# A 31-tap convolution as 8-phase Toeplitz matmuls through DRAM scratch, with batched LayerNorm and a block-wise first phase

## Chip, cores, metric

One Trainium2 chip, all 8 cores, each running the same program on its own share: one prompt sequence of 2048 positions and 16 of the 128 sample requests (4 tokens each), 2112 columns a core in blocks of 512, 512, 512, 512 and 64. The time of a run is the device time of its slowest core, in microseconds (us). Some executions of any kernel here fall into a slower state, in which the cores of one die show a lower granted TensorE clock; only fast runs are compared below.

## The reference, cut

Two layers; each is RMSNorm, one input projection into 56 column tiles of 128, two groups of 8 heads, one output projection, residual. The change concerns group A:

```python
def hybrid_layer(x, buf_a, buf_b, norm_g, w_in, conv_a_w, conv_a_b, ln_a_g, ln_a_b, conv_b_w, w_out):
    h = rmsnorm(x, norm_g)
    p = jnp.einsum('btd,de->bte', h, w_in)                           # (B, T, D_IN)
    # [cut: split into a_val, a_gate, z_a, gb, gc, hb, z_b]
    # group A: Conformer convolution module
    u = a_val * jax.nn.sigmoid(a_gate)                               # GLU
    ca, new_a = causal_dwconv(u, buf_a, conv_a_w)                    # width 31, depthwise
    ca = head_layernorm(ca + conv_a_b, ln_a_g, ln_a_b)               # over 128 channels, per token
    y_a = jax.nn.silu(ca) * jax.nn.silu(z_a)
    # [cut: group B, short convolution of width 3 with gates]
    y = jnp.einsum('bte,ed->btd', jnp.concatenate([y_a, y_b], axis=-1), w_out)
    return x + y, new_a, new_b
```

## The kernel before, as far as the change touches it

Channels are on partitions and positions along the free dimension. Each engine runs its operations in the order in which the program lists them; a helper turns the listed reads and writes into semaphore waits. `pop_rank` and `defer` place the later stages of one step among the matmuls of the next.

```python
def a_step(l, j, b, jj, slots):                 # one head j, one block b
    mm_group(bg, n, [... w_gate, h ...]); pop_rank(1)            # g projection, 8 matmuls
    # ... tanh on ScalarE, v projection, u = (tanh+1)*v on VectorE into ubuf ...
    mm_group(bz, n, [... w_z, h ...])                            # z projection
    # ... silu(z) on ScalarE ...
    def pe_fn(e):                                                # taps 12..30: diagonal matmuls
        for i, k in enumerate(pe_taps):
            ins = e.matmul(banks[bd][:, 0:n], lhsT=mk[:, ms, k, :], rhs=usl(k), start=(i == 0), ...)
    def dve_taps(k0, k1):                                        # taps 0..11: multiply-adds on VectorE
        # ... two chains of scalar_tensor_tensor over usl(k) ...
    def stage0():   # two merges on TensorE with the centring matrix cb16; Square on ScalarE
    def stage1():   # variance: matmul with ones
    def stage2():   # Ln, Exp on ScalarE; tt = (centred + bias) * rstd on VectorE
    def stage3():   # s = silu(gain*tt + bias) on ScalarE
    def stage4():   # y = s * silu(z) on VectorE
    for rk, fn in enumerate([stage0, stage1, stage2, stage3, stage4]):
        defer(sid, rk, fn)
# [cut: start: x in blocks; every block normalised before the first projection]
# [cut: 4 output rounds a layer, 4 heads each]
```

## Time and profile before

| | before |
|---|---|
| median (fast runs) | 1615.1 us (1614.3 to 1616.2, 4 runs) |
| spans of the cores | 1606.2 to 1615.4 us |
| mean granted TensorE clock by core | 0.962 to 0.973 |
| TensorE busy, VectorE busy | 1433 us, 1229 us |
| table loads on ScalarE | 165 |

The engine totals, the groups and the unbroken runs of matmuls are shown in the prediction. Two further lines of the page: the granted clock in forty equal slices, in tenths of full speed, and the traffic.

```profile
PEclk9999999999999999999989999999999999999997
...
HBM read 92.20 MB, written 13.37 MB: 65 GB/s over the span
```

The clock was nearly full throughout, 0.97 in the mean on this core. To compare kernels I also took the start of every matmul of one core from the trace. The gap to the next start, less the cost of that matmul when it runs unbroken (0.216 us for 512 columns, 0.1425 for 336, 0.029 for 64, all from the prediction; the middle one is an estimate there), is what a wait or a cold clock added. Before, on core 3: 10.1 us ahead of the first matmul + 1363.6 of matmul by count + 222.1 added + 19.6 after the start of the last one = 1615.4 us.

### The profile page before, as it was taken

What the parts mean: (1) busy time and instruction counts of PE and PEld (TensorE: products, weight loads), DVE (VectorE), ACT (ScalarE), POOL (GpSimd) and SP (SyncE); (2) the same over time, 40 slices, a digit from 0 to 9 for tenths busy, and PEclk for the clock granted to TensorE, in tenths of its full rate; (3) what the DMA queues carried; (4) which work ended last, traced back from release to release, by engine and by line L of the source; (5) the groups of instructions that cost most, each with busy time, mean ns of one, the idle gap of its engine ahead of it and who ended that gap; (6) DMA issues with size and microseconds to landing.
All of it is one profiled execution on the core that took longest, in us unless ns stands there. A gap on an engine that the chain in (4) does not pass through costs nothing.

```text
span 1615.4 us, 23509 instructions; the slowest of 8 cores (1606.2 to 1615.4 us)
## 1 busy us (share of the span) xinstructions
PE 1433.3 (89%) x7642; PEld 652.0 (40%) x7642; DVE 1229.2 (76%) x2240; ACT 622.8 (39%) x896; POOL 78.6 (5%) x148
## 2 busy tenths in 40 slices
PE   2399998999999999999979999899998999999983
PEld 0144443444444444444434444444444444444431
DVE  1589998899896556655699999889998665655566
ACT  2346665266652111111245666436665111011133
POOL 1000000000000010010000000000000010000000
PEclk9999999999999999999989999999999999999997
DMA  7801111111112131122411011111111222113116
GB/s 191 190 12 22 26 27 20 33 27 27 21 20 37 27 53 27 27 42 38 39 33 20 12 22 26 21 33 27 26 21 20 37 34 46 27 27 53 21 38 184
DMA packets 43253, 65.91 MB, mean 41 GB/s; under 512 B 14016, under 2 KB 16320, under 8 KB 43072
## 3 DMA queue, kind: packets, MB, share of 16 engines
q0 software_dynamic: 20736, 37.76, 14.7%
q1 hardware_dynamic: 22400, 26.67, 6.5%
q8 instruction: 64, 1.05, 0.3%
q14 instruction: 53, 0.43, 0.1%
HBM read 92.20 MB, written 13.37 MB: 65 GB/s over the span
## 4 chain that ended last, share of the span: by engine, by line
PE 73%; issue 9%; DVE 8%; ACT 5%; DMA 4%; SPq 1%; DVEq 0%; ACTq 0%
PE psb L360 58%; PE psb L517 13%; DMA x_sb<-xT 3%; ACT L563 2%; DVE h_sb L404 1%; DVE acc L538 1%; PE psb L550 1%; ACT rstd_t L565 1%; DVE vbuf L630 1%; ACT lnv_t L563 1%; DVE accb L538 1%; DVE y_sb L578 1%; ACT sq L382 1%; PE psb L389 1%; DVE acc L535 1%
## 5 line engine op out<-in xcount | busy, mean ns | idle before, releaser
L360 PE MATMUL psb<-h_sb,wsl 128*128 128x512 bf16 (+1 forms) x4480 | 839.4, 345 | 19.8 <-DVE vbuf L630 12.0
L360 PEld LDWEIGHTS psb<-h_sb,wsl 128*128 128x128 bf16 x4480 | 381.0, 98 | 456.0 <-issue 42.7
L538 DVE SCALAR_TENSOR_TENSOR acc<-ubuf,cwh,acc 128x512 f32<-128x512 bf16 (+1 forms) x640 | 371.1, 652 | 0.5 <-DVE acc L538 0.3
L517 PE MATMUL psb<-ubuf,mk 128*128 128x512 bf16 (+1 forms) x1520 | 289.5, 346 | 12.7 <-DVE ubuf L479 7.5
L360 PE MATMUL psb<-y_sb,wsl 128*128 128x512 bf16 (+1 forms) x1280 | 250.9, 355 | 14.2 <-DVE x_sb L429 6.1
L429 DVE TENSOR_TENSOR x_sb<-x_sb,psb 128x512 f32<-128x512 f32 (+1 forms) x320 | 181.2, 592 | 43.6 <-PE psb L360 41.6
L517 PEld LDWEIGHTS psb<-ubuf,mk 128*128 128x128 bf16 x1520 | 129.8, 99 | 161.8 <-issue 21.7
L630 DVE TENSOR_TENSOR vbuf<-psb,tt_t 128x512 bf16<-128x512 f32 (+1 forms) x80 | 47.7, 597 | 164.9 <-PE psb L360 164.9
L360 PEld LDWEIGHTS psb<-y_sb,wsl 128*128 128x128 bf16 x1280 | 112.1, 100 | 148.5 <-issue 40.4
L616 ACT ACTIVATE sz_t<-psb 128x512 f32<-128x512 f32 (+1 forms) x80 | 41.9, 523 | 284.2 <-PE psb L360 284.2
L574 ACT ACT_TABLE_LOAD x80 | 102.6, 1283 | 85.7 <-DVE tt_t L567 85.7
L471 ACT ACTIVATE th_t<-psb 128x512 f32<-128x512 f32 (+1 forms) x80 | 41.8, 523 | 228.6 <-PE psb L360 228.4
L623 ACT ACTIVATE tt_t<-psb 128x512 f32<-128x512 f32 (+1 forms) x80 | 41.8, 523 | 210.7 <-PE psb L360 203.0
L654 DVE SCALAR_TENSOR_TENSOR acc<-vbuf,cw_b_sb,acc 128x512 f32<-128x512 bf16 (+1 forms) x160 | 105.3, 658 | 17.4 <-DVE acc L651 0.9
L563 ACT ACT_TABLE_LOAD x80 | 102.6, 1283 | 23.5 <-PE psb L360 21.7
L343 POOL DMA_DIRECT2D wsl<-w_in_r x112 | 61.0, 556 | 970.5 <-PE psb L360 947.0
L538 DVE SCALAR_TENSOR_TENSOR accb<-ubuf,cwh,acc 128x512 bf16<-128x512 bf16 (+1 forms) x160 | 97.7, 652 | 0.0
L389 PE MATMUL psb<-sq,ones_s 128*128 128x512 bf16 (+1 forms) x120 | 38.2, 426 | 56.1 <-ACT sq L382 56.0
L382 ACT ACTIVATE sq<-x_sb 128x1024 bf16<-128x1024 f32 (+1 forms) x60 | 51.5, 898 | 79.0 <-PE psb L389 35.9
L404 DVE SCALAR_TENSOR_TENSOR h_sb<-x_sb,vecs_sb,rstd_t 128x512 bf16<-128x512 f32 (+1 forms) x80 | 46.5, 654 | 42.2 <-ACT rstd_t L397 42.1
L550 PE MATMUL psb<-accb,cb 128*128 128x512 bf16 (+1 forms) x160 | 44.7, 345 | 36.3 <-DVE accb L538 36.3
L567 DVE SCALAR_TENSOR_TENSOR tt_t<-psb,cbias,rstd_t 128x512 f32<-128x512 f32 (+1 forms) x80 | 52.4, 655 | 24.6 <-ACT rstd_t L565 24.2
(44 smaller groups left out, 714.3 us busy)
## 6 DMA issues: line engine op xcount, KB each, us to landing
wsl<-w_in_r POOLq DMA_DIRECT2D x112, 256.0 KB, 5.5
x_sb<-xT SPq DMA_DIRECT2D x4, 2048.0 KB, 31.8
wsl<-w_out_r POOLq DMA_DIRECT2D x32, 256.0 KB, 4.4
y_fm<-sz_t SPq DMA_DIRECT2D x18, 256.0 KB, 2.2
hista<-hist_a SPq DMA_DIRECT2D x16, 240.0 KB, 2.6
y_fm<-th_t SPq DMA_DIRECT2D x14, 256.0 KB, 2.2
oa_copy<-sa_orig SPq DMA_DIRECT2D x2, 1664.0 KB, 23.0
oa_new<-oa_t SPq DMA_DIRECT2D x2, 256.0 KB, 12.6
```

Source lines behind the costliest of these rows:

```text
L343: P.op("pool", (lambda e, i=i, s=s: e.dma_start(out=wsl[:, s, :], in_=wseq[i])), reads=([x_r[0][0]] if i == 0 else []), writes=[w_r[s]], c ...
L360: ins = e.matmul(outap, lhsT=l_, rhs=r_, start=(i == 0), stop=(i == len(pairs) - 1))
L382: P.op("act", (lambda e, s=s, kp=kp, c0=c0, n=n: e.activation(out=sq[:, s, :, 0:n], in_=x_sb[:, 2 * kp:2 * kp + 2, c0:c0 + n], func=AF.Squ ...
L404: P.op("dve", (lambda e, k=k, c0=c0, n=n: e.scalar_tensor_tensor(out=h_sb[:, k, c0:c0 + n], in0=x_sb[:, k, c0:c0 + n], scalar=vecs[:, gcol ...
L429: P.op("dve", (lambda e, bk=bk, m=m, c0=c0, n=n: e.tensor_tensor(out=x_sb[:, m, c0:c0 + n], in0=x_sb[:, m, c0:c0 + n], in1=banks[bk][:, 0: ...
L517: ins = e.matmul(banks[bd][:, 0:n], lhsT=mk[:, ms, k, :], rhs=usl(k), start=(i == 0), stop=(nd == 0 and i == len(pe_taps) - 1))
L538: P.op("dve", (lambda e, k=k, wcol=wcol, outap=outap, c=c: e.scalar_tensor_tensor(out=outap, in0=usl(k), scalar=wcol, in1=acc[:, c, 0:n], ...
L550: P.op("pe", (lambda e, c=c, ci=ci: e.matmul(banks[bd][:, 0:n], lhsT=cb16[:], rhs=accb[:, 2 * iac + c, 0:n], start=False, stop=(ci == len( ...
L563: P.op("act", (lambda e: e.activation(out=lnv_t[:, 0, 0:n], in_=banks[bvv][:, 0:n], func=AF.Ln, bias=LN_EPS)), reads=[bank_r[bvv]], writes ...
L574: P.op("act", (lambda e: e.activation(out=ss_t[:, 0, 0:n], in_=tt_t[:, 0, 0:n], func=AF.Silu, scale=gcol, bias=bcol)), reads=[tt_r, const_ ...
L630: P.op("dve", (lambda e: e.tensor_tensor(out=vout, in0=banks[bhb][:, 0:n], in1=gcs_t[:, 0, 0:n], op=ALU.mult)), reads=[bank_r[bhb], gcs_r] ...
L654: P.op("dve", (lambda e, k=k, wcol=wcol: e.scalar_tensor_tensor(out=acc[:, iac, 0:n], in0=vsl(k), scalar=wcol, in1=acc[:, iac, 0:n], op0=A ...
```

## The change

Its intent: take 12 taps off VectorE and make the taps on TensorE cheaper. With 16 channels x 8 phases of the position on the 128 partitions, one head's convolution is 8 channel groups x 5 shifts, each a dense 128x128 Toeplitz matmul of 336 columns. Getting into this layout and back needs two trips through DRAM scratch per head. LayerNorm is batched over a head (its two Exp follow one another, so few table changes), and the first three heads start block by block as x is normalised. A bank, below, is one of the eight buffers in which TensorE leaves its results (psb in the profiles). The diff, cut to its core:

```diff
-        def pe_fn(e):            # 19 diagonal taps a block; dve_taps: 12 on VectorE
+    def conv_lnstat(l, cj, lj, nxt):          # conv of head cj beside the statistics of head lj
+        for g in range(8):
+                mm_group(bk, banks[bk][:, 0:UROW],
+                         [(toep[:, half, (gg * NSH + s) * 128:(gg * NSH + s + 1) * 128], up_sb[:, g, 64 - 16 * s:UPROW - 16 * s])
+                          for s in range(NSH)], [toep_r[half], up_r, uph_r], f"conv{cj}.{g}")
+                # [cut: eviction to co_sb, store to scr_c after each half]
+                if 2 <= g < 7:
+                    ln_var(g - 2)             # ones matmul, Ln
+                if g < 5:
+                    ln_center(l, lj, g)       # centring matmul, Square
+        up_load(l, nxt); hist_load(l, nxt)
+        # [cut: two Exp over rs_t; load of cn_sb from scr_c]
+    def ln_out(l, j, slot):
+        for q in range(NB):
+            P.op("dve", ...)                  # tt: rs = (centred + bias) * rs
+            P.op("act", ...)                  # s:  rs = Silu(gain*rs + bias)
+            bz = proj(sw, q, pw, f"z{j}.{q}") # z projection, banks 0 to 2
+            P.op("act", ...)                  # sz: Silu(z)
+            P.op("dve", ...)                  # y:  rs * sz
+            pop()                             # one background job
+        def prep(j):                          # background jobs of the next head
+            bg.append(hist_scale)             # waits for the history load
+            bg.append(lambda: build(j, 0))    # Toeplitz tiles
+            bg.append(lambda: build(j, 1))
-    def rms_phase(gcol0, final=False):        # all blocks first
+        for q in range(NB):
+            for j in range(3):
+                p1_block(l, j, q, UB[j], sl[j])
+                if l == 0 and q + 1 < NB:
+                    if j == 0:
+                        # [cut: squares, sums, rstd of block q+1]
+                        for k in range(KC):
+                            bg.append(lambda q=q, k=k: rms_apply(0, q + 1, k))
+                    if j == 2:
+                        pop(8)
# [cut: the last two output rounds merged over 8 heads, next layer's sums and h inside]
```

## The prediction

> **What bounds the kernel now.** I read the engine totals first, then the groups with the shapes kept apart, then the chain in order of time and stretches of the timeline, because a share of busy time is an average over stages. The page's engine totals and the head of its chain:
>
> ```profile
> PE 1433.3 (89%) x7642; PEld 652.0 (40%) x7642; DVE 1229.2 (76%) x2240; ACT 622.8 (39%) x896; POOL 78.6 (5%) x148
> ...
> PE 73%; issue 9%; DVE 8%; ACT 5%; DMA 4%; SPq 1%; DVEq 0%; ACTq 0%
> ```
>
> TensorE is the bound: 89% busy, and 73% of the chain that ended last. Its three largest groups in the table with shapes kept apart (busy us, mean ns, then idle before):
>
> ```profile
> L360 PE MATMUL psb<-h_sb,wsl 128*128 128x512 bf16 x3584 | 807.5, 383 | 14.4 <-DVE vbuf L630 12.0 <-DVE ob_t L636 2.3
> L517 PE MATMUL psb<-ubuf,mk 128*128 128x512 bf16 x1216 | 275.6, 381 | 7.5 <-DVE ubuf L479 7.5
> L360 PE MATMUL psb<-y_sb,wsl 128*128 128x512 bf16 x1024 | 238.9, 394 | 8.0 <-DVE vbuf L630 6.1 <-issue 1.0 <-DVE x_sb L429 0.6
> ```
>
> The second is the 19 of 31 conv taps that run as diagonal matmuls; the other 12 run on VectorE. A mean of 380 ns is the latency of one pipelined matmul, not its cost. The cost is read from unbroken runs, one in the chain in order of time and two in the timeline (start, duration, what):
>
> ```profile
> 571.43 26.05 PE psb L360 x120
> ```
>
> ```profile
> 69.04 7.01 PE L360 MATMUL psb<-h_sb,wsl 128*128 128x512 bf16 x24
> ...
> 117.92 0.63 PE L360 MATMUL psb<-h_sb,wsl 128*128 128x64 bf16 x16
> ```
>
> 120 wide ones take 26.05 us: less one drain, (26.05-0.38)/119 = 0.216 us each. Sixteen of 64 columns: (0.63-0.19)/15 = 0.029 us. The line at 69.04 is the first projection. It starts only at 69 us, since the program normalises every block first, and 24 matmuls take 7.0 us instead of 5.4: a cold start. So before has 6112 x 0.216 + 1528 x 0.029 = 1364 us of matmul in 1615 us; 69 us are the start, and a group-A head takes 45.6 us (starts at 97.76, 143.38, 189.23 in the chain) against 41.1 us of matmul, a group-B head 30.4 (571.43, 601.83) against 28.6.
>
> **What the Trainium skill says.** (1) "TensorE: Matmul & The Clock Gate", section Wait — 56ns, not 53.3ns?: back to back a warm matmul costs N/2.4 ns plus about 2.5. The trace agrees (0.216, 0.029), so I use it for the new 336-column matmuls: 142.5 ns, an estimate. (2) Same page, The HAM clock gate: after an idle window of about 3.4 us the array runs at half clock until it has been busy about as long. The trace agrees: the first eight of those 24 are spaced 0.43 us, and a gap of 2 us at 120 us slowed nothing. (3) "VectorE: DVE Perf Modes", The perf-mode tier table: a tensor_tensor on bf16 in SBUF runs at two elements per cycle, on fp32 at one. Before has only the fp32 case, the diagonal build, 2432 elements in 2684 ns; the bf16 case is not in it. (4) "ScalarE: Activation LUTs", What ACT_TABLE_LOAD costs: a load of 1283 ns plus a drain of about 1380. The trace has 1283, but the Silu at 105.06 starts when the load of 103.76 ends: no drain.
>
> **The change, part by part.** *Matmuls.* A conv over (16 channels x 8 phases) needs 5 shifts of 8 groups per head: 16 x 40 = 640 matmuls of 336 columns instead of 1520 taps; 160 merges become 80 centrings. Left: 4832 x 0.216 + 1208 x 0.029 + 640 x 0.1425 = 1043 + 35 + 91 = 1170 us. **Removed: 195 us** on the bounding engine.
>
> *VectorE* loses the taps, about 531 us, and 43 us of diagonal builds. It gains 128 evictions of 336 columns (estimate 0.5 us from 686 ns for 512 PSUM columns, 64 us in all) and 32 Toeplitz builds of 2560 bf16 elements (estimate 1.5 us by (3), 48 us). It falls to some 780 us, far from a bound by its sum.
>
> *ScalarE* loses most of 160 table loads (205 us); about 40 remain.
>
> *DMA* gains 4 trips of 688 KB for each of 16 heads, 44 MB. Queues are nearly idle in the middle (12 to 53 GB/s against about 190 at the ends), and a trip has some 16 us or more to land.
>
> *Start.* x comes in two halves, block 0 is normalised alone, and three heads start by block. x0 lands near 14 us (before: 2 MB in 13.4 us from its issue), then squares, sum, Ln, Exp 4.8 us and eight h of 0.66: matmuls begin near **25 us** instead of 69. Blocks of x follow each 10 us, three heads use 10.4 us per block: I add 4 us for late weights.
>
> *Layer boundary and end.* The last two output rounds are merged with sums and h inside them; before, the last one of layer 1 spans 783 to 836 for 29 us of matmul. I allow 3 us at the boundary, 13 us after the last output matmul (sums, Ln, Exp, eight outputs of 0.66, one store), 5 us in all 16 B heads and 2 us around the first conv.
>
> *The new wait.* Here I expect much of the gain to go. The order of the program decides: for each block the new LayerNorm output issues on VectorE tt(q), y(q), and on ScalarE s(q), sz(q). VectorE is in order, so tt(q+1) stands behind y(q), which needs sz(q), which stands behind s(q), which needs tt(q). That is a loop through two engines, with these durations in the groups of before:
>
> ```profile
> L567 DVE SCALAR_TENSOR_TENSOR tt_t<-psb,cbias,rstd_t 128x512 f32<-128x512 f32 x64 | 47.9, 749 | 24.2 <-ACT rstd_t L565 24.0
> L574 ACT ACTIVATE ss_t<-tt_t,vecs_sb 128x512 f32<-128x512 f32 x64 | 52.1, 814 | 0.8
> L498 ACT ACTIVATE sz_t<-psb 128x512 f32<-128x512 f32 x64 | 37.1, 579 | 19.7 <-PE psb L360 19.7
> L578 DVE TENSOR_TENSOR y_sb<-ss_t,sz_t 128x512 bf16<-128x512 f32 x64 | 44.0, 687 | 4.4 <-ACT ss_t L574 4.4
> ```
>
> With about 0.1 us of hand-over (in the trace Exp ends at 102.82, tt starts at 102.93) and as much overlap back to back, one turn is 2.8 us, while its projection needs 1.73 us. Two Toeplitz builds and a history scaling sit in the same stretch on VectorE. From the end of the conv: Exp over 1024 and 1088 columns (estimate 1.06 and 1.11 from 630 ns at 512, 256 ns at 64) to 1.7, table load to 3.0, s0, sz0 to 4.35, y0 5.1, scaling 5.35, sz1 7.4, build 9.6, sz2 11.65, build 13.8, sz3 15.9, tt4 16.9, sz4 17.5. The projections use only three banks, so the five end at 7.75 instead of 7.1. The next projection takes bank 0, held until sz3, or bank 2 then 3, held until sz2 and tt4. TensorE stands until about 16 us: **8 to 9 us lost** per head, 5.5 to 7 for the last two, which build nothing. Per layer 9.0+8.2+8.9+8.2+8.9+8.9+5.5+7.1 = 65 us. An idle time of 8 us also cools the clock: 2 us per head, 16 us. In the conv itself five squares (678 ns), five Ln (597 ns) and a table load on ScalarE take longer than 7.5 us of matmul: 1.6 us for seven heads, 5 us where the last head has no conv beside it: 16 us. Per layer 97 us, in both **194 us**.
>
> Sum: 25 + 1169 + 4 + 194 + 5 + 3 + 2 + 13 = 1415; I say **1412 us**, 12.6% less.
>
> **Rivals.** *Hidden chain.* If the waits are covered, TensorE is left at 1170 + 25 + 13 and small losses: some 1240 us. For it: every sum of an engine is well below 1170. Against: the in-order loop above, and so few free banks. *Slow build.* If the broadcast operands keep the builds at one element per cycle, as the fp32 one of before, each is 2.8 us; 12 of the 16 heads have them in the chain: 12 x 2.6 = 31 us, 1445 us. *Transfers.* If the trip through DRAM (672-byte runs, write then read) took 15 us or more each way, the conv of the third head, which has no other head between, and the first would wait: perhaps 10 us each per layer, 1440 us. Before moves few short packets in volume, so its trace cannot exclude it. *Clock.* Fewer pauses could mean a lower grant; in the densest stretches of before it was 1.00, which speaks against it.
>
> **Range and chances.** The removed matmuls and the earlier start are nearly certain (195 + about 40 us). The chain is worked out from durations, but its start may shift by 1 us per head and the cold clock may be half or double: 30 us together; the slow build and the transfers push up 30, a chain partly covered pulls down 60. Hence 1345 to 1475. To miss 2% the losses would have to be 360 us instead of 194: 0.96 faster, 0.03 same, 0.01 slower.
>
> **What would show it.** Right: about 1170 us of matmul by count, first projection near 25 us, VectorE near 780, about 40 table loads; projections after each LayerNorm output waiting on ScalarE's sz or on VectorE's tt, 6 to 9 us per head, and a clock near 0.5 after it; A heads of 38 to 43 us. Wrong: TensorE waits on DMA into the phase-layout or normalised tile (then it is the transfers), builds of 2.8 us, no idle stretch around the z projections (then near 1240), or a first projection after 35 us.

## The result, and the profile after

| | before | after |
|---|---|---|
| fast runs | 1615.1 us (median) | 1533.1 and 1535.6 us |
| slow runs | none in this pair | 1633.2 (die 0 at clock 0.84), 1712.3 (die 1 at 0.79) |
| ratio, fast runs | 1 | 0.950 [0.948, 0.952] |
| spans of the cores | 1606 to 1615 | 1514 to 1532 |
| granted clock by core | 0.962 to 0.973 | 0.924 to 0.927 |

Ratios here and below are the mean time of one kernel's fast runs over that of the other's in the same rounds, so not quite the ratio of the medians quoted. The change is 5% faster; the direction was foreseen, the size was not: 1412 was predicted with a range to 1475. The page of after, engine totals, clock, traffic and head of the chain:

```profile
PE 1257.2 (82%) x6558; PEld 582.7 (38%) x6682; DVE 713.0 (47%) x1293; ACT 497.8 (33%) x807; POOL 140.2 (9%) x268
...
PEclk9998878898989899999989989889898989999998
...
HBM read 116.85 MB, written 35.14 MB: 99 GB/s over the span
...
PE 69%; DMA 9%; DVE 8%; issue 7%; ACT 6%; DVEq 0%; POOL 0%; ACTq 0%; POOLq 0%; SPq 0%
```

TensorE and VectorE both shed work as meant (124 matmul records of this core are missing, the weight loads count 6682), but the clock now dips again and again, and TensorE stands in many places; e9 tests whether one comes of the other. What TensorE and the two engines that serve it wait for, from the view of waits (engine and line, whom it waited for, total us, times, longest):

```profile
ACT rs_t L549 <- DVE rs_t L546: 164.7, 64, 6.4
PE psb L318 <- ACT sz_t L553: 139.5, 30, 8.4
...
DVE up_sb L457 <- DMA up_sb<-hist_a: 52.8, 14, 10.1
...
PE psb L318 <- DMA wsl<-w_in_r: 30.5, 4, 9.9
...
PE psb L318 <- DVE h_sb L396: 15.5, 4, 4.6
```

The second line is the new wait that the prediction named. The third is one that it didn't: `hist_scale` on VectorE waits for its load. One LayerNorm output, timeline of all engines (start, duration, what, then in brackets the idle time before and its releaser); the conv before it ends at 285.3:

```profile
285.80 0.75 DVE L546 SCALAR_TENSOR_TENSOR rs_t<-psb,cbias,rs_t 128x512 f32<-128x512 f32 x1
285.81 0.96 POOL L454 DMA_DIRECT2D up_sb<-hist_a  x1 [7.79 <-PE psb L318]
...
286.70 1.28 ACT L549 ACT_TABLE_LOAD   x1
...
288.00 0.82 ACT L549 ACTIVATE rs_t<-rs_t,vecs_sb 128x512 f32<-128x512 f32 x1
...
288.72 0.57 ACT L553 ACTIVATE sz_t<-psb 128x512 f32<-128x512 f32 x1
289.40 0.69 DVE L555 TENSOR_TENSOR y_sb<-rs_t,sz_t 128x512 bf16<-128x512 f32 x1 [2.85 <-ACT sz_t L553]
294.44 0.29 DVE L457 TENSOR_SCALAR up_sb<-up_sb 128x512 bf16<-128x512 bf16 x1 [4.35 <-DMA up_sb<-hist_a]
294.64 0.74 DVE L546 SCALAR_TENSOR_TENSOR rs_t<-psb,cbias,rs_t 128x512 f32<-128x512 f32 x1
295.49 0.81 ACT L549 ACTIVATE rs_t<-rs_t,vecs_sb 128x512 f32<-128x512 f32 x1 [6.19 <-DVE rs_t L546]
```

Read it as a chain. The history load is issued at 285.81, when the conv has released its buffer. VectorE finishes y(0) at 290.1 and stands 4.35 us for that load, 8.6 us after its issue; only then may it run tt(1), for which ScalarE has stood 6.19 us. TensorE in the same stretch (timeline of TensorE alone):

```profile
285.29 7.07 PE L318 MATMUL psb<-h_sb,wsl 128*128 128x512 bf16 x31
296.92 0.59 PE L318 MATMUL psb<-h_sb,wsl 128*128 128x64 bf16 x8 [4.57 <-ACT sz_t L553]
301.27 3.57 PE L318 MATMUL psb<-h_sb,wsl 128*128 128x512 bf16 x8 [3.77 <-ACT sz_t L553]
306.51 12.71 PE L318 MATMUL psb<-h_sb,wsl 128*128 128x512 bf16 x71 [1.66 <-DVE rs_t L546]
```

Ten microseconds of standing, and the eight matmuls at 301.27 take 3.57 us, where eight warm ones take 8 x 0.216 + 0.17 = 1.9. The beginning of the program (TensorE alone):

```profile
26.66 3.57 PE L318 MATMUL psb<-h_sb,wsl 128*128 128x512 bf16 x8 [8.50 <-DMA wsl<-w_in_r]
34.55 3.58 PE L318 MATMUL psb<-h_sb,wsl 128*128 128x512 bf16 x8 [4.33 <-DMA wsl<-w_in_r]
...
53.36 4.93 PE L318 MATMUL psb<-h_sb,wsl 128*128 128x512 bf16 x16 [4.58 <-DVE h_sb L396]
...
122.26 15.41 PE L318 MATMUL psb<-h_sb,wsl 128*128 128x512 bf16 x71 [9.92 <-DMA wsl<-w_in_r]
```

The first projection starts at 26.7 us, close to the predicted 25; the normalised block is ready at 25.1 (VectorE's last h of block 0), so its weights cost the rest. Three of the four later blocks stand 4.3 to 4.6 us for h, the last 2.2, and the fourth head 9.9 us for weights.

**Where the time went.** I used core 6, which has all 6682 matmul records (the two cores with missing records would show false gaps), and the same method as for before: 13.3 + 1169.1 of matmul + 336.4 added + 10.0 = 1528.8 us. So the change removed 195 us of matmul, as computed, and gave 114 us of it back in added gaps. (That the last difference in the table is 114 too is chance.) By stage, with the terms of the prediction in the same sorting; the prediction gave no time for the first matmul, so the measured 13 is taken out of its 25 us to the first projection (its terms sum to 1415, for which it said 1412):

| stage (core 6, us) | predicted | measured | difference |
|---|---|---|---|
| before the first matmul | 13 | 13.3 | 0 |
| matmul by count | 1169 | 1169.1 | 0 |
| start, to the fourth head's projections | 16 (25 - 13 + 4) | 57.3 | +41 |
| conv with statistics, and around the first conv | 34 (2 x 16 + 2) | 59.4 | +25 |
| LayerNorm outputs, cold clock with them | 162 (2 x 65 + 2 x 16) | 175.8 | +14 |
| weights of layer 2's fourth head | 0 | 8.9 | +9 |
| layer boundary | 3 | 14.7 | +12 |
| end, last output round and after | 13 | 25.4 | +12 |
| the rest (B heads and others) | 5 | 4.8 | 0 |
| sum | 1415 | 1528.7 | +114 |

### The profile page after: what moved, and what is told of

Its sections match the earlier page's. It is cut to its first block, busy times and chain, and to the rows that moved or that the text cites. A ratio compares the mean times of both kernels' runs of the same rounds, so it can differ in the third digit from the quotient of the medians.

```text
span 1531.5 us, 20107 instructions; the slowest of 8 cores (1513.9 to 1531.5 us)
## 1 busy us (share of the span) xinstructions
PE 1257.2 (82%) x6558; PEld 582.7 (38%) x6682; DVE 713.0 (47%) x1293; ACT 497.8 (33%) x807; POOL 140.2 (9%) x268
## 3 DMA queue, kind: packets, MB, share of 16 engines
q1 hardware_dynamic: 47456, 65.82, 13.3%
## 4 chain that ended last, share of the span: by engine, by line
PE 69%; DMA 9%; DVE 8%; issue 7%; ACT 6%; DVEq 0%; POOL 0%; ACTq 0%; POOLq 0%; SPq 0%
PE psb L318 68%; DMA up_sb<-hist_a 6%; DMA wsl<-w_in_r 2%; DVE toep L470 2%; DVE rs_t L546 2%; ACT sz_t L553 2%; ACT sq L364 2%; PE psb L378 1%; DVE x_sb L620 1%; DVE y_sb L555 1%; DVE h_sb L396 1%; ACT rs_t L526 1%; DMA x_sb<-x_d 1%; ACT sq L518 0%; ACT rs_t L549 0%
## 5 line engine op out<-in xcount | busy, mean ns | idle before, releaser
L620 DVE TENSOR_TENSOR x_sb<-x_sb,psb 128x512 f32<-128x512 f32 (+1 forms) x240 | 139.6, 593 | 82.5 <-PE psb L318 79.9
L318 PE MATMUL psb<-y_sb,wsl 128*128 128x512 bf16 (+1 forms) x785 | 157.6, 343 | 3.4 <-DVE x_sb L620 2.3
L318 PE MATMUL psb<-up_sb,toep 128*128 128x336 bf16 x640 | 114.6, 315 | 25.0 <-ACT sz_t L553 12.2
L597 DVE SCALAR_TENSOR_TENSOR rs_t<-vbuf,cw_b_sb,rs_t 128x512 f32<-128x512 bf16 (+1 forms) x160 | 104.9, 656 | 26.8 <-POOL vbuf L580 17.5
L549 ACT ACTIVATE rs_t<-rs_t,vecs_sb 128x512 f32<-128x512 f32 (+1 forms) x80 | 59.0, 738 | 164.9 <-DVE rs_t L546 164.7
L555 DVE TENSOR_TENSOR y_sb<-rs_t,sz_t 128x512 bf16<-128x512 f32 (+1 forms) x80 | 47.9, 599 | 129.4 <-ACT sz_t L553 129.4
L487 DVE CAST co_sb<-psb 128x336 bf16<-128x336 f32 x128 | 64.3, 507 | 66.7 <-PE psb L318 66.3
L318 PEld LDWEIGHTS psb<-up_sb,toep 128*128 128x128 bf16 x640 | 58.5, 99 | 71.2 <-issue 43.8
L518 ACT ACTIVATE sq<-psb,cbias 128x512 bf16<-128x512 f32 (+1 forms) x80 | 49.3, 619 | 76.9 <-PE psb L318 76.8
L318 PE MATMUL psb<-y_sb,toep 128*128 128x512 bf16 (+1 forms) x314 | 70.3, 348 | 0.3
L396 DVE SCALAR_TENSOR_TENSOR h_sb<-x_sb,vecs_sb,rs_t 128x512 bf16<-128x512 f32 (+1 forms) x80 | 49.5, 653 | 28.1 <-ACT rs_t L390 28.1
```

Source lines behind the costliest of these rows:

```text
L318: ins = e.matmul(out, lhsT=l_, rhs=r_, start=(i == 0), stop=(i == len(pairs) - 1))
L396: P.op("dve", (lambda e: e.scalar_tensor_tensor(out=hv(k, q), in0=xv(k, q), scalar=vecs[:, gcol0 + k:gcol0 + k + 1], in1=rv, op0=ALU.mult, ...
L487: P.op("dve", (lambda e, bk=bk, half=half, gg=gg: e.tensor_copy(co_sb[:, half, gg, :], banks[bk][:, 0:UROW])), reads=[bank_r[bk]], writes= ...
L518: P.op("act", (lambda e: e.activation(out=sq[:, s, 0:n], in_=banks[bk][:, 0:n], func=AF.Square, bias=cbias[:, col:col + 1])), reads=[bank_ ...
L549: P.op("act", (lambda e, r_ap=r_ap: e.activation(out=r_ap, in_=r_ap, func=AF.Silu, scale=gcol, bias=bcol)), reads=[rs_r[q], vecs_r], write ...
L555: P.op("dve", (lambda e, r_ap=r_ap, iz=iz, n=n, q=q: e.tensor_tensor(out=y_ap(slot, q), in0=r_ap, in1=sz_t[:, iz, 0:n], op=ALU.mult)), rea ...
```

## The experiments

All gave correct results. Kernels e1 to e4, e5 to e8, and e9 with e10 each shared a chip and runs of before (fast medians of before 1616.0 to 1616.1). "After" below is 1534 us, ratio 0.950.

| run | edit against after | median of fast runs | ratio [95%] |
|---|---|---|---|
| e1 | history scaling behind the two builds | 1489.1 | 0.922 [0.920, 0.923] |
| e2 | all tt ahead of the loop | 1381.6 | 0.856 [0.854, 0.857] |
| e3 | both | 1362.8 | 0.843 [0.841, 0.845] |
| e4 | all blocks normalised first | 1514.1 | 0.938 [0.936, 0.941] |
| e5 | e3 + e4 + fourth head's weights early | 1337.9 | 0.828 [0.827, 0.829] |
| e6 | e3 + by block with h early + weights early | 1345.1 | 0.831 [0.830, 0.833] |
| e7 | weights early alone | 1527.7 | 0.945 [0.944, 0.947] |
| e8 | each scratch load twice | 1567.9 | 0.970 [0.969, 0.972] |
| e9 | 28 useless matmuls behind each LayerNorm output | 1512.0 | 0.936 [0.933, 0.939] |
| e10 | e5 + first builds earlier | 1338.4 | 0.827 [0.825, 0.830] |

**e1: is it the history load?** Two theories for the standing of TensorE: the loop tt, s, sz, y alone, or the load in front of it.

```diff
         def prep(j):
-            bg.append(hist_scale)
             bg.append(lambda: build(j, 0))
             bg.append(lambda: build(j, 1))
+            bg.append(hist_scale)
```

> Only the history scaling is put behind the two Toeplitz builds in the deferred list. In the changed kernel VectorE waited 52.8 us for that load (14 waits, 3.8 us each), in the middle of the tt-s-sz-y loop. Theory (the loop sets when TensorE may go on, and the load's 8.6 us sit in it): 12 heads have it in the loop, about 4 us each, so 45 to 55 us less: 1478 to 1490 us, and the wait before the next projection falls from 8 to 4-5 us. Rival (VectorE at 47% is not the bound; its wait covers other waits): within 10 us of 1534.

Measured 1489, 45 us less. In the view of waits VectorE's wait for the history load falls from 52.8 to 6.3 us, and TensorE waits less for ScalarE:

```profile
PE psb L318 <- ACT sz_t L553: 98.8, 26, 7.2
...
PE psb L318 <- DVE up_sb L457: 10.1, 2, 5.1
```

So the position of one 0.3 us operation cost 45 us. The second line is the price of moving it: in both layers the third head's conv now waits for the scaling. What remains, 98.8 us, should be the loop; e2 and e3 test that. One detail of the expectation was missed: the wait before the next projection fell less than to 4 to 5 us (in layer 1 from 8.2 to 7.0 us ahead of the seventh head's first one).

**e2 and e3: the loop itself.** All five tt before anything else; s, sz and y then follow without VectorE standing between two tt.

```diff
         for q in range(NB):
             P.op("dve", ...)    # tt(q)
+        for q in range(NB):
             P.op("act", ...)    # s(q), then z projection, sz(q), y(q), pop()
```

> Only the order of emission in the LayerNorm output: all five tt on VectorE first, then s, projection, sz, y by block. The history wait stays where it is. Theory: tt(q+1) no longer stands behind y(q), the loop through two engines is cut; sz3 falls from about 20 us after the conv to 11 (y1 still stands behind the history load, and the gate tile has two buffers): 8 to 9 us in 12 heads, 6 to 7 in 4, some of the cold clock with it: 100 to 140 us less, 1395 to 1435 us. Rival (three banks, not the order, hold TensorE): under 40 us less.

> Both of the above. Theory: LayerNorm output runs at the pace of its projections, 1.73 us a block; what stays is the table load at its head. 12 us less in 12 heads, 6 in 4, and the granted clock back to about 0.97: 1330 to 1380 us, about the sum of the two single ones or a little less. Rival (another wait takes their place: the phase-layout load or the normalised tile's load, which have then only 8 us in the third head): more than 1420 us with TensorE waiting for up_sb or cn_sb.

Measured 1382 for e2 (152 us less, somewhat more than expected) and 1363 for e3 (171 less, as expected). The two edits overlap: e1's 45 us shrink to 19 once the tt are out of the loop, since the history wait then holds back only y. One LayerNorm output of e3, conv ended at 224.7 (timeline of all engines; the lines of other operations are left out):

```profile
224.71 7.30 PE L318 MATMUL psb<-h_sb,wsl 128*128 128x512 bf16 x40
...
225.30 2.91 DVE L546 SCALAR_TENSOR_TENSOR rs_t<-psb,cbias,rs_t 128x512 f32<-128x512 f32 x5
...
232.67 14.44 PE L318 MATMUL psb<-h_sb,wsl 128*128 128x512 bf16 x80 [0.66 <-ACT sz_t L556]
```

One stop of 0.66 us where after had 4.57, 3.77 and 1.66. By stage on core 6, LayerNorm outputs add 14.4 us in e3, against 32.5 in e2, 137.3 in e1 and 175.8 in after; the clock by core is back at 0.961 to 0.978. This is the same arithmetic in another order on VectorE. The rival of e3's expectation shows itself too, in small: with the loop gone, TensorE waits at the second and third heads for loads from scratch, of the phase layout and of the conv's result, for which after never waits:

```profile
PE psb L318 <- DMA up_sb<-scr_u: 6.1, 1, 6.1
...
PE psb L318 <- DMA cn_sb<-scr_c: 2.5, 3, 1.2
```

**e4: what the by-block start is worth.** It undoes that part of the change: the normalisation of all blocks first, as before.

```diff
-            for kp in range(4):
-                rms_mm(0, kp, rms_sq(0, kp))
-            # ... rstd and h of block 0
+            for q in range(NB):
+                # ... squares, sums, rstd, h of block q
-                if l == 0 and q + 1 < NB:
+                if False:
```

> Undoes one part of the change: all five blocks are normalised before the first projection, as before; the three first heads still go by block. In the changed kernel the three heads' first phase ended at 112.3 us (27 us start plus 86 us for 47 us of matmul). Theory (by-block start gave back nearly all it won, through late weights, h of the next block and a cold clock at each block): first projection near 65 us, phase ended near 110, total within 12 us of 1534. Rival (the early start pays its 40 us as predicted): 1565 to 1580 us.

A miss on the good side: 1514, 20 us faster than after. TensorE alone at the start:

```profile
43.97 43.81 PE L318 MATMUL psb<-h_sb,wsl 128*128 128x512 bf16 x216
...
100.49 14.97 PE L318 MATMUL psb<-h_sb,wsl 128*128 128x512 bf16 x72 [9.80 <-DMA wsl<-w_in_r]
```

The first projection starts 17 us later than in after, but runs unbroken, and the phase ends at 90.7 instead of 112.3. The statistics of all five blocks are done at 44 us here, not at 69 as in before; the changed layout of x, in which a block is one contiguous piece, may be why, but no run tells that apart. The by-block start, from which I had expected 44 us, costs 20 us as written.

**e7: weights early alone.** The fourth head's weights are requested ahead of the three halo copies on GpSimd (they copy the edge positions that neighbouring pieces of the sequence share), which wait for the last block and stand before the request in its queue.

```diff
         pop(len(bg))
+        s3 = w_get(("in", l, 8 + 3), ("in", l, 3))
         for j in range(3):
             p1_end(l, j, UB[j])
```

> The changed kernel with only the weight request of the fourth head moved ahead of the halo copies. Theory (GpSimd's queue is in order, the request waits behind copies that wait for the last block; it then lands 9.5 us after its issue beside three stores): the waits of 9.9 and 7.8 us fall to about 4 to 6 each: 1522 to 1530 us. Rival (the slot of the ring is what it waits for): nothing, 1532 to 1536 us.

Measured 1527.7, within the expectation, but only some 6 us of the 18 or so that the two waits took: they fall from 9.9 and 7.8 to 3.3 and 2.6 us, but TensorE's waits for VectorE's copies of the last positions of u (the new state that the layer returns) grow from 3.3 to 9.7 us. VectorE's waits show what stands behind two of them:

```profile
DVE u_sb L426 <- DMA scr_u<-u_sb: 25.4, 2, 13.4
```

The fourth head writes its u into the first head's buffer, and so waits until that head's store to scratch has landed. After shows no such wait: there the weights come later than the store. So the store side of the trips, which e8 below does not touch, is the next limit here.

**e5 and e6: can the by-block start be mended?** Both have e3's order and early weights. e5 normalises first; e6 keeps the blocks but issues the next h at once, ahead of the evictions of the second and third head.

```diff
                         for k in range(KC):
-                            bg.append(lambda q=q, k=k: rms_apply(0, q + 1, k))
-                    if j == 2:
-                        pop(8)
+                            rms_apply(0, q + 1, k)
```

> Both reorderings of the LayerNorm output, all blocks normalised before the first projection, and the two weights of the fourth head asked for before the halo copies of the first three are queued on GpSimd. Theory: the parts are independent, so 1364 minus 20 (first phase ends at 90 instead of 112) minus 5 to 10 (two weight waits of 9.5 and 8 us halved): 1330 to 1342 us. Rival (the start's gain was tied to the late chain): no better than 1355 us.

> As the last, but the start stays by block and only the order is mended: the eight h of the next block are issued on VectorE before the u of this block's second head, instead of behind the u of its third. Theory (h of the next block stands behind u of the third head on VectorE, 4.5 us and a cold clock at each block): the four gaps of 2 to 4.5 us go, first phase ends near 90, 1330 to 1345 us in all. Rival (late weights of the first block are what costs): the first phase ends at 105 or later, over 1350 us.

e5 came in at 1338, as expected; e6 at 1345.1, at the upper end. In e6 the stops before each block shrink and the clock holds:

```profile
51.11 3.61 PE L318 MATMUL psb<-h_sb,wsl 128*128 128x512 bf16 x16 [1.54 <-DVE h_sb L396]
```

3.61 us for 16 matmuls is warm, where after had 4.93 behind a stop of 4.58. That bears out the cause: in after five of the eight h of the next block stood on VectorE behind u of the third head, which waits for TensorE. But e6 still waits 9.5 and 4.2 us for its first weights, which e5 doesn't feel. e5 is the best version found, 17% below before (e10, below, equals it).

**e8: are the trips through DRAM hidden?** Each load of the two scratch tiles is done twice, so that each trip takes longer; the stores stay as they are.

```diff
-        P.op("sp", ... up_sb <- scr_u ...)
+        for _ in range(2):
+            P.op("sp", ... up_sb <- scr_u ...)
# [the same for cn_sb <- scr_c]
```

> The changed kernel with each load from the DRAM scratch done twice, the second after the first (about 9 us more for the phase-layout tile and for the normalised tile, 18 us per head). Theory (the trips are hidden except where less than 27 us lie between two convs, the second and third head of each layer): 35 to 60 us more, all at those heads, none elsewhere: 1570 to 1595 us. Rival (the trip is on the path of every head): about 16 x 18 = 290 us more.

Measured 1567.9: 34 us more, just under the low end of the expectation and far from what it would be if every trip were on the path. The new waits of TensorE:

```profile
PE psb L318 <- DMA cn_sb<-scr_c: 20.2, 4, 7.3
...
PE psb L318 <- DMA up_sb<-scr_u: 14.0, 5, 4.9
```

20.2 + 14.0 is as much as the 34 us, and all nine waits are at the first three heads of a layer. Elsewhere even doubled loads are hidden. In after itself TensorE never waits for either tile (median 9.5 and 8.6 us from issue to landing).

**e9: what is the cold clock worth?** The loop stays; 28 matmuls into a bank that is free at that point follow each LayerNorm output, so TensorE computes rubbish where it would stand. Their result is never read.

```diff
+        mm_group(4, banks[4][:, 0:512], [(wsl[:, sw, 0:128], hv(k % KC, 0)) for k in range(28)],
+                 [w_r[sw]] + [h_r[k][0] for k in range(KC)], f"warm{j}")
```

> The changed kernel with 28 matmuls of no use (6 us, into a bank that is free by then) at the end of each head's z projections, where TensorE else stands 4 to 8 us. No wait is taken away. Theory (the idle stretch cools the clock, and the next projection's first 8 matmuls cost 3.6 us instead of 1.7): nothing is waited for less, but the matmuls after it run warm: 15 to 30 us less, 1503 to 1519 us, granted clock up from 0.926 to 0.95 or more. Rival (the restart is hidden behind the next wait for a bank, or the clock follows something else): within 6 us of 1534, or slower.

Measured 1512, 22 us less with 448 matmuls more, as expected. The mean clock of the cores rises from 0.925 to between 0.954 and 0.968. The same place in after, then in e9 (TensorE alone):

```profile
259.90 16.59 PE L318 MATMUL psb<-h_sb,wsl 128*128 128x512 bf16 x79 [8.21 <-ACT sz_t L553]
```

```profile
261.20 14.45 PE L318 MATMUL psb<-h_sb,wsl 128*128 128x512 bf16 x80 [0.64 <-ACT sz_t L553]
```

80 projections take 14.45 us instead of 16.6 (one of the 80 records is missing in after). So 22 us of cold clock, net of what the useless matmuls cost, can be had back in this way, of the 36 counted around LayerNorm outputs; better is not to stand, as e3 does.

**e10: earlier builds on top of e5.**

```diff
+            if q == 3:
+                prep(0)         # in the first phase, instead of after it
```

> The best so far (both reorderings, all blocks normalised first, weights early) with the first head's Toeplitz builds issued during the first phase instead of in the fourth head, where the u of its first block stands behind 2.9 us of builds (TensorE waited 8.1 us for VectorE there in two places). Theory: 5 to 8 us less than 1338: 1330 to 1334 us. Rival (the fourth head's conv waits for the phase-layout load anyway): 1336 to 1340 us, the wait moved to up_sb.

No change (1338.4), as its rival said. TensorE still waits 9.6 us for the copies of the last positions of u, now with no build in front of them: VectorE stands there for the store of the first head's u, as in e7 (25.4 us in two waits, 22.1 in e5). It also waits 8.6 us for the phase layout, 7.6 of them at the third head of layer 1. One more buffer for u, or an earlier store, was not tried.

## Why the prediction was right or wrong

**Right.** What bounds the kernel, and the matmul: 1169 us by count, and a B head takes 28.6 us of 28.9 predicted. The Toeplitz builds take 1484 ns for 2560 elements (1.5 us estimated), about twice the rate of before's fp32 build (2432 in 2684 ns), so the rival of the slow build fell, and the 336-column evictions take 507 ns of 0.5 us. Both rows, from the groups with shapes kept apart:

```profile
L470 DVE TENSOR_TENSOR toep<-mask_sb,wt_sb 128x2560 bf16<-128x2560 bf16 x32 | 47.2, 1484 | 0.0
...
L487 DVE CAST co_sb<-psb 128x336 bf16<-128x336 f32 x128 | 64.3, 507 | 66.7 <-PE psb L318 66.3
```

Table loads fell to 45 (40 predicted). The fourth A head takes 42.2 us from conv to conv in layer 1 and 43.4 in layer 2 (core 6; 38 to 43 predicted). VectorE fell further than said, to 713 instead of 780; 42 us of that is the 80 residual adds that the merged output round saves (181.2 to 139.6 us), which I had overlooked. The rival of the transfers fell for this kernel: TensorE waits for neither tile, and e8's doubled loads cost 34 us in all; in e3, without the loop, 8.6 us of such waits come to light. The rival of the hidden chain fell by the waits of after; e3 shows what it would have taken. The rival of the clock fell too: with fewer pauses the grant rose (0.925 in after, 0.961 to 0.978 in e3).

**Right in mechanism and in sum, wrong inside: the new wait.** The step "per layer 65 us" plus "2 us per head" of cold clock, 162 us in both, was measured at 175.8 on core 6. That the sum came so near is luck: two errors cancelled. The step "y0 5.1, scaling 5.35" gave the history scaling its 0.3 us of work and forgot that its load is issued only when the conv ends; it stood 4 us there, and e1 cut the stage's added time by 38.5 us (175.8 to 137.3). The loop without it stops TensorE for 105 us (e1), not 130: I had priced it about a quarter too dear. The cold part, 36 us of 32, was right.

**Wrong in size: the start.** "I add 4 us for late weights" and matmuls from 25 us on gave 16 us of added time; it was 57. By then the first two sets of weights, the h of each block behind another head's eviction, the fourth head's weights and a cold array came on top. I checked that each block of x lands in time, and not what stands ahead of each h on VectorE or each weight request on GpSimd. e4, e6 and e7 each take a piece of it away.

**Wrong in size: the small terms.** "Per layer 16" for conv with statistics (34 with the first conv) was 59. Away from the third head it was right, 28.5 us of 29 in both layers on core 6. The third head's conv, where no projection lies between it and the LayerNorm output, added 20.4 us instead of 3.2: the loop runs on into it. (In e3 it still adds 15.6, there with the waits for loads from scratch.) "2 us around the first conv" was about 10; 4.7 of them are the fifth head of layer 1, where VectorE stood 10.1 us for the history load, and e1 leaves 0.3 of these. "3 us at the boundary" was 15. "13 us after the last output matmul" was right (12.5), but another 13 came before it: TensorE waits for the squares of the residual inside the merged round of each layer, 24 us in 32 stops of at most 2.2 us over the whole program, those at the start included. I had assumed that those sums hide. Layer 2's fourth head waits 8 us for weights, a term I did not have.

**The range.** It allowed 60 us upward, for the chain, the builds and the transfers. The sums of these three held; but 100 of the 114 us came from five terms (the start, the conv, layer 2's weights, the boundary, the end) that together stood at 66 us and measured 166, and to which I gave no uncertainty at all.

## What to carry to other kernels

When work moves between in-order engines, write down for each stage the queue of every engine, transfers' issue points with them: one 0.3 us operation inside a loop cost 45 us here, and the order of five others 150. An early start is a gain only if the stream behind it is unbroken; e4, which starts 17 us later, ends 20 us sooner. And where a prediction is a sum, the terms set to "a few us" need a range too: here all that were off erred in the same direction.

## What the Trainium skill lacked or had wrong

- "TensorE: Matmul & The Clock Gate", The HAM clock gate: agrees (eight matmuls after a stop of 3.77 us take 3.57 us instead of 1.9), but doesn't say what filling unavoidable stops with useless matmuls is worth: 22 us of 1534 in e9, with the mean clock from 0.925 to about 0.96.
- "ScalarE: Activation LUTs", What ACT_TABLE_LOAD costs: the drain of about 1380 ns doesn't show here. In after the load of 286.70 takes 1.28 us and the Silu starts at 288.00.
- "DMA: Bandwidth & Descriptors", Anatomy of one DMA: the fit of about 2.0 us plus bytes over the bandwidth gives an estimate of 2.3 us for a load of 128 KB; the same page says that pieces under 512 B are slower, but has no time for such a load. The history load, issued by GpSimd, cast from 32 to 16 bits on the way and written in rows of 128 bytes, took 7.0 us in the median, and 8.6 until VectorE was released in the stretch shown. How far short rows, the cast or other traffic make it longer isn't told apart by these runs.
- No page that I read tells how to price a loop through two in-order engines (tt, s, sz, y); it stood for 105 us of TensorE's stops in e1, and reordering it saved 152 us in e2.
